# A gated unit on one core: three slots packed in place, one instruction per tile and engine, and small stores at the start

## Chip, cores and metric

One core of a Trainium2 chip. The metric is the device time of one execution in microseconds (us), the median of several runs. The profile comes from one traced execution; its span is about 2 us shorter than the time.

## The reference

```python
x = np.random.randn(8192, 8192).astype(np.float32)

def reference(x):
    a, b = np.split(x, 2, axis=-1)
    return a * (1 / (1 + np.exp(-b)))
```

268 MB are read and 134 MB written; there is one sigmoid and one multiply per result. Nothing is read twice.

## The kernel before

The 8192 rows are cut into 32 tiles. A tile has two rows per partition: 64 KB per partition in, 32 KB out. Loads are issued by SyncE (SP). Stores are issued by ScalarE (ACT), whose queue also holds the sigmoids. VectorE (DVE) multiplies.

```python
R = 2
pool = ctx.enter_context(tc.tile_pool(name="io", bufs=2))
for i in range(n_tiles):
    x_sb = pool.tile([P, R * n_cols], fp32)
    o_sb = pool.tile([P, R * half], fp32)
    load = nc.sync.dma_start(out=x_sb, in_=x_t[i])
    n = 4 if i == n_tiles - 1 else 1        # the last tile in pieces
    w = half // n
    for r in range(R):
        for c in range(n):
            ...                             # a, b: one row's halves; cols: its place in o_sb
            nc.scalar.activation(out=b, in_=b, func=SIG)
            nc.vector.tensor_mul(out=o_sb[:, cols], in0=a, in1=b)
            if n > 1:
                nc.scalar.dma_start(out=out_t[i, :, cols], in_=o_sb[:, cols])
    if n == 1:
        nc.scalar.dma_start(out=out_t[i], in_=o_sb)
```

The order in which instructions stand in each engine's queue is made by a scheduler from this program; it need not be the program's order. At the end the first load is moved into the entry block.

Of the kernel before, what the change touches and what calls it, by code (L numbers as in the profile page):

```python
# [1 line left out]

# [4 lines left out]


def _tiles(ctx, tc, x, out):
    nc = tc.nc  # L10
    P = nc.NUM_PARTITIONS
    fp32 = mybir.dt.float32
    SIG = mybir.ActivationFunctionType.Sigmoid

    n_rows, n_cols = x.shape
    half = n_cols // 2
    R = 2
    n_tiles = n_rows // (P * R)
    x_t = x.rearrange("(n p r) m -> n p (r m)", p=P, r=R)
    out_t = out.rearrange("(n p r) m -> n p (r m)", p=P, r=R)  # L20

    pool = ctx.enter_context(tc.tile_pool(name="io", bufs=2))
    first = None

    for i in range(n_tiles):
        x_sb = pool.tile([P, R * n_cols], fp32)
        o_sb = pool.tile([P, R * half], fp32)
        load = nc.sync.dma_start(out=x_sb, in_=x_t[i])
        first = first or load
        n = 4 if i == n_tiles - 1 else 1  # L30
        w = half // n
        for r in range(R):
            for c in range(n):
                lo = r * n_cols + c * w
                a = x_sb[:, lo : lo + w]
                b = x_sb[:, lo + half : lo + half + w]
                cols = slice(r * half + c * w, r * half + (c + 1) * w)
                nc.scalar.activation(out=b, in_=b, func=SIG)  # L38
                nc.vector.tensor_mul(out=o_sb[:, cols], in0=a, in1=b)  # L39
                if n > 1:  # L40
                    nc.scalar.dma_start(out=out_t[i, :, cols], in_=o_sb[:, cols])  # L41
        if n == 1:
            nc.scalar.dma_start(out=out_t[i], in_=o_sb)
    return first


@with_exitstack
def kernel(
    ctx: ExitStack,
    tc: tile.TileContext,  # L50
    x: bass.AP,
    out: bass.AP,
):



    nc = tc.nc
    with ExitStack() as pools:
        _tiles(pools, tc, x, out)
    tc.close()  # L60
    tc.compile()  # L61
    blocks = nc.main_func.blocks
    entry, body = blocks[0].instructions, blocks[1].instructions
    SP = mybir.EngineType.SP
    at = next(k for k, i in enumerate(body) if i.engine == SP)
    load = body[at]
    assert load.opcode == "DMACopy" and not load.sync_info.on_wait
    del body[at]
    where = next(k for k, i in enumerate(entry) if i.engine == SP and i.opcode == "Drain")
    entry.insert(where, load)  # L70


# [1 line left out]
_INS = ['x']  # L74
_OUTS = [((8192, 4096), 'float32')]


# [23 lines left out]
```

## Time and profile before

| | before |
|---|---|
| time, median of 6 runs | 936.12 us (935.98 to 937.0) |
| span of the profiled run | 933.9 us |
| DMA engines busy, loads + stores | 66.5% + 33.3% |
| VectorE, ScalarE busy | 30%, 25% |
| rate in the steady part | 434 GB/s |

The first thing to read is the DMA row, which says 9 in every slice. The kernel is a copy with a little arithmetic beside it, and the only time to be won is that in which the 16 DMA engines are not at full rate. The prediction shows the lines.

### The profile page before, as it was taken

The page shows a single profiled execution, that of the slowest core. Times are in us where ns is not written, and L with a number is a line of the kernel's source. Part 1 is how long each engine was busy: PE and PEld are TensorE (multiplying, and loading weights), DVE is VectorE, ACT ScalarE, POOL GpSimd, SP SyncE. Part 2 cuts the span into 40 slices and gives each one's busy share as a digit, 9 for nine tenths or more (in the row PEclk, how much of TensorE's full clock was granted, in tenths as well). Part 3 has the DMA queues.
Part 4 walks back from the last instruction along what each step waited for, and adds up shares of the span by engine and source line. Part 5 has one row for each costly group of instructions (what it writes and reads, how often), then busy time and mean ns, then how long its engine had stood idle before and what let it go on. Part 6 is the DMA issues. An engine that isn't in the chain of part 4 may idle for free.

```text
span 933.9 us, 410 instructions
## 1 busy us (share of the span) xinstructions
DVE 280.9 (30%) x70; ACT 230.0 (25%) x71; POOL 0.2 (0%) x4
## 2 busy tenths in 40 slices
DVE  0333321333213333133331333312333123331234
ACT  1313331133311333203332033320233202333023
POOL 0000000000000000000000000000000000000000
DMA  9999999999999999999999999999999999999998
GB/s 404 420 434 431 453 418 429 439 434 449 420 456 404 452 424 427 449 425 451 412 459 410 438 438 425 451 421 452 413 449 421 431 445 443 429 420 453 410 446 362
DMA packets 10226, 402.67 MB, mean 431 GB/s; under 512 B 1136, under 2 KB 1136, under 8 KB 2160
## 3 DMA queue, kind: packets, MB, share of 16 engines
q1 hardware_dynamic: 4608, 268.44, 66.5%
q10 hardware_dynamic: 5616, 134.22, 33.3%
q14 instruction: 2, 0.02, 0.0%
HBM read 268.44 MB, written 134.22 MB: 431 GB/s over the span
## 4 chain that ended last, share of the span: by engine, by line
DMA 78%; DVE 15%; ACT 6%; issue 0%; DVEq 0%; ACTq 0%
DMA x_sb<-in_x_dram 78%; DVE o_sb L39 15%; ACT x_sb L38 6%; DVEq L61 0%; ACTq L41 0%; ACTq L38 0%
## 5 line engine op out<-in xcount | busy, mean ns | idle before, releaser
L39 DVE TENSOR_TENSOR o_sb<-x_sb 128x4096 f32<-128x4096 f32 (+1 forms) x70 | 280.9, 4056 | 647.2 <-ACT x_sb L38 647.2
L38 ACT ACTIVATE x_sb<-x_sb 128x4096 f32<-128x4096 f32 (+1 forms) x70 | 228.7, 3315 | 695.9 <-DMA x_sb<-in_x_dram 691.8
L38 ACT ACT_TABLE_LOAD x1 | 1.3, 1283 | 0.8 <-PEq L85 0.8
L85 POOL MEMSET const-uint8-127<- 128x1 uint8 x1 | 0.1, 103 | 0.0
L85 POOL MEMSET const-bfloat16-1.0<- 128x1 bf16 x1 | 0.1, 102 | 0.0
L85 POOL MEMSET const-float32-0.0<- 128x1 f32 x1 | 0.1, 99 | 0.2 <-issue 0.2
L85 POOL MEMSET const-float32-1.0<- 128x1 f32 x1 | 0.1, 99 | 0.0
## 6 DMA issues: line engine op xcount, KB each, us to landing
out_dram<-o_sb ACTq DMA_DIRECT2D x31, 4096.0 KB, 41.7
out_dram<-o_sb ACTq DMA_DIRECT2D x8, 512.0 KB, 6.2
x_sb<-in_x_dram SPq DMA_DIRECT2D x32, 45.5
```

The source lines that it names most:

```text
L38: nc.scalar.activation(out=b, in_=b, func=SIG)
L39: nc.vector.tensor_mul(out=o_sb[:, cols], in0=a, in1=b)
L85: nc = _bacc.Bacc("TRN2", target_bir_lowering=False, num_devices=1)
```

## The change

The intent: a single 64 KB slot per partition holds a tile's input and, packed into its first half, its result, so that three tiles fit where two pairs of buffers did; each tile has one sigmoid and one multiply; 128 KB of small stores go out at the start, so that the store queue is in use until the first result is ready; the last tile is loaded in halves and stored in larger pieces.

```diff
-    pool = ctx.enter_context(tc.tile_pool(name="io", bufs=2))
+    pool = ctx.enter_context(tc.tile_pool(name="slots", bufs=1))
+    slots = [pool.tile([P, R * n_cols], fp32, name=f"slot{k}") for k in range(SLOTS)]
+    def implied(later, *earlier):            # drops a wait that follows from another
+        for e in earlier:
+            tc.declare_no_dep(later.ins, e.ins, reason="follows from the wait that is kept")
+    nc.vector.memset(blank, 0.0)
+    nc.scalar.dma_start(
+        out=out_t[n_tiles - 1, :, :256].rearrange("p (k m) -> p k m", k=2),
+        in_=blank.to_broadcast([P, 2, 128]))
...
+        rows = slot.rearrange("p (r h m) -> p r h m", r=R, h=2)
+        packed = slot[:, : R * half].rearrange("p (r m) -> p r m", r=R)
+        def load(cols):
+            ins = nc.sync.dma_start(out=slot[:, cols], in_=x_t[i, :, cols])
+            implied(ins, *(e for e in gone if e not in awaited))   # awaited: the slot's last stores
+        def glu(r, c):
+            sig = nc.scalar.activation(out=rows[:, r, 1, c], in_=rows[:, r, 1, c], func=SIG)
+            mul = nc.vector.tensor_mul(out=packed[:, r, c], in0=rows[:, r, 0, c], in1=rows[:, r, 1, c])
+            implied(sig, *gone); implied(mul, *gone, *now["loads"])
+            if i == n_tiles - 1:
+                tc.keep_in_program_order(sig)
...
+        if i < n_tiles - 1:
+            load(slice(0, R * n_cols))
+            glu(slice(0, R), every)
+            ...                              # one store; two for the last tile but one
+        else:                                # last tile: two loads, row 1 in halves, two stores
```

More of the change, by code (lines that the diff above doesn't have):

```diff
@@ L13, in _tiles @@
     SIG = mybir.ActivationFunctionType.Sigmoid
+    SLOTS = 3
     n_rows, n_cols = x.shape
@@ L20, in _tiles @@
     out_t = out.rearrange("(n p r) m -> n p (r m)", p=P, r=R)
-    pool = ctx.enter_context(tc.tile_pool(name="io", bufs=2))
-    first = None
-    for i in range(n_tiles):
-        x_sb = pool.tile([P, R * n_cols], fp32)
-        o_sb = pool.tile([P, R * half], fp32)
-        load = nc.sync.dma_start(out=x_sb, in_=x_t[i])
-        first = first or load
-        n = 4 if i == n_tiles - 1 else 1
-        w = half // n
-        for r in range(R):
-            for c in range(n):
-                lo = r * n_cols + c * w
-                a = x_sb[:, lo : lo + w]
-                b = x_sb[:, lo + half : lo + half + w]
-                cols = slice(r * half + c * w, r * half + (c + 1) * w)
-                nc.scalar.activation(out=b, in_=b, func=SIG)
-                nc.vector.tensor_mul(out=o_sb[:, cols], in0=a, in1=b)
-                if n > 1:
-                    nc.scalar.dma_start(out=out_t[i, :, cols], in_=o_sb[:, cols])
-        if n == 1:
-            nc.scalar.dma_start(out=out_t[i], in_=o_sb)
@@ L44, in _tiles @@
-    return first
+    pool = ctx.enter_context(tc.tile_pool(name="slots", bufs=1))
[3 more added lines that the diff above has]
+            tc.declare_no_dep(later.ins, e.ins, reason="follows from the wait that is kept")
+    blank = ctx.enter_context(tc.tile_pool(name="blank", bufs=1)).tile([P, 1, 128], fp32)
+    nc.vector.memset(blank, 0.0)
+    nc.scalar.dma_start(
+        out=out_t[n_tiles - 1, :, :256].rearrange("p (k m) -> p k m", k=2),
+        in_=blank.to_broadcast([P, 2, 128]),
+    )
@@ new lines, in _tiles, with store @@
+    kinds = ("loads", "sigs", "muls", "stores")
+    history = [{k: [] for k in kinds} for _ in range(SLOTS)]
+    last_stores = [[] for _ in range(SLOTS)]
+    every = slice(0, half)
+    for i in range(n_tiles):
+        slot = slots[i % SLOTS]
+        old = history[i % SLOTS]
+        now = {k: [] for k in kinds}
+        gone = sum(old.values(), [])
+        awaited = last_stores[i % SLOTS]
+        rows = slot.rearrange("p (r h m) -> p r h m", r=R, h=2)
[3 more added lines that the diff above has]
+            implied(ins, *(e for e in gone if e not in awaited))
+            now["loads"].append(ins)
+        def glu(r, c):
+            sig = nc.scalar.activation(out=rows[:, r, 1, c], in_=rows[:, r, 1, c], func=SIG)
+            mul = nc.vector.tensor_mul(
+                out=packed[:, r, c], in0=rows[:, r, 0, c], in1=rows[:, r, 1, c]
+            )
+            implied(sig, *gone)
+            implied(mul, *gone, *now["loads"])
+            if i == n_tiles - 1:
+                tc.keep_in_program_order(sig)
+            now["sigs"].append(sig)
+            now["muls"].append(mul)
+        def store(cols):
+            ins = nc.scalar.dma_start(out=out_t[i, :, cols], in_=slot[:, cols])
+            implied(ins, *(e for e in gone if e not in old["stores"]), *now["loads"], *now["sigs"])
+            now["stores"].append(ins)
+        if i < n_tiles - 1:
+            load(slice(0, R * n_cols))
+            glu(slice(0, R), every)
+            n_stores = R if i == n_tiles - 2 else 1
+            w = R * half // n_stores
+            for k in range(n_stores):
+                store(slice(k * w, (k + 1) * w))
+        else:
+            for r in range(R):
+                load(slice(r * n_cols, (r + 1) * n_cols))
+            for r in range(R):
+                halves = [slice(0, half // 2), slice(half // 2, half)]
+                for c in [every] if r == 0 else halves:
+                    glu(slice(r, r + 1), c)
+                store(slice(r * half, (r + 1) * half))
+        for k in kinds:
+            old[k] += now[k]
+        last_stores[i % SLOTS] = now["stores"]
@@ L64 @@
     SP = mybir.EngineType.SP
-    at = next(k for k, i in enumerate(body) if i.engine == SP)
+    at = next(k for k, i in enumerate(body) if i.engine == SP and i.opcode == "DMACopy")
     load = body[at]
```

## The prediction

> **What bounds the kernel now.** I read the page's busy lines first, then the DMA digits, the queue table, stretches of the run one by one, and last the chain of waits.
>
> ```profile
> span 933.9 us, 410 instructions
> DVE 280.9 (30%) x70; ACT 230.0 (25%) x71; POOL 0.2 (0%) x4
> ...
> DMA  9999999999999999999999999999999999999998
> ...
> q1 hardware_dynamic: 4608, 268.44, 66.5%
> q10 hardware_dynamic: 5616, 134.22, 33.3%
> ...
> HBM read 268.44 MB, written 134.22 MB: 431 GB/s over the span
> ```
>
> VectorE and ScalarE are idle 70% of the span and more, while the 16 DMA engines are busy in every slice. The two queues' packets, loads (q1) and stores (q10), fill 66.5 + 33.3 = 99.8% of the engines' time. A kernel like this gains only if it moves fewer bytes, moves them faster, or closes the 0.2%.
>
> To see where speed is lost I cut the span at the places where the traffic changes: loads alone, loads with stores, the end. Columns: stretch, length, three engines' busy time, clock, DMA share, GB/s.
>
> ```profile
> 4.10:37.90 33.80, 8.76 (x2) 7.12 (x2) 0.00 (x0) 1.00 1.00 432
> 37.90:41.50 3.60, 0.00 (x0) 0.00 (x0) 0.00 (x0) 1.00 1.05 319
> ...
> 0.00:41.50 41.50, 8.76 (x2) 8.41 (x3) 0.20 (x4) 1.00 0.98 407
> 41.50:99.50 58.00, 17.52 (x4) 14.24 (x4) 0.00 (x0) 1.00 1.00 434
> 99.50:911.50 812.00, 245.31 (x56) 199.44 (x56) 0.00 (x0) 1.00 1.00 434
> 911.50:933.90 22.40, 9.35 (x8) 7.90 (x8) 0.00 (x0) 1.00 0.88 372
> ```
>
> Loads alone run at 432 GB/s and loads mixed with stores at 434, the same rate. A tile is 8.39 MB in and 4.19 MB out, 12.58 MB, so at 434 GB/s it takes 29.0 us, and 32 tiles take 32 x 29.0 = 928 us. The span is 933.9, so only 5.9 us are not full-rate traffic. The table says where. In the first 41.5 us, 407 GB/s moved 16.9 MB, worth 38.9 us: 2.6 us lost. In the last 22.4 us, 372 GB/s moved 8.33 MB, worth 19.2 us: 3.2 us lost. Of the first loss about 1.0 us is one event: between 37.9 and 41.5, where the first stores join the loads, the rate falls to 319, and 3.6 x (434 - 319)/434 = 0.95 us. The other 1.6 us are the issue of the first load and its slow first packets.
>
> ```profile
> 0.79 42.87 DMA x_sb<-in_x_dram
> 43.66 0.02 issue
> 43.68 3.62 ACT x_sb L38
> 47.31 0.02 issue
> 47.33 8.77 DVE o_sb L39 x2
> 56.12 45.52 DMA x_sb<-in_x_dram
> ```
>
> The chain of waits looks like a latency chain: landing, sigmoid, two multiplies, next load. It would tempt one to say that the compute, 12.4 us of every 58, is on the path. It is not. The load issued at 56.12 takes 45.5 us for bytes that take 19.3 us alone, because it stands behind other transfers; the compute is hidden behind a full DMA queue.
>
> ```profile
> out_dram<-o_sb ACTq DMA_DIRECT2D x31, 4096.0 KB, 41.7
> x_sb<-in_x_dram SPq DMA_DIRECT2D x32, 45.5
> L39 DVE TENSOR_TENSOR o_sb<-x_sb 128x4096 f32<-128x4096 f32 x62 | 271.6, 4422 | 626.6 <-ACT x_sb L38 626.6
> L38 ACT ACTIVATE x_sb<-x_sb 128x4096 f32<-128x4096 f32 x62 | 220.8, 3608 | 670.1 <-DMA x_sb<-in_x_dram 670.1
> ```
>
> **What the Trainium skill says.** "DMA: Bandwidth & Descriptors", section "Where 436 GB/s comes from", puts the ceiling of the 16 engines at 435.2 GB/s, and says that for HBM to SBUF a limit of about 358 binds first. The trace sides with the first: 434 sustained for 870 us on this lone core. The steady state therefore cannot be improved by the change; it is within 0.3% of the ceiling.
>
> The same page, section "Queues, rings and completion order", says that an engine takes turns between the rows it has work for, packet by packet. The trace agrees only in part. If turns began at issue, a 4 MB store beside loads would need about 29 us; it takes 41.7 from issue to landing. The other 13 us I read as transfers issued earlier going first. So I work the new order out first come, first served, and test the tail also with turns.
>
> "VectorE: DVE Perf Modes", section "The TRN2 errata", gives (N+151)/0.96 ns for an fp32 two-tensor operation: 4,424 for 4,096 columns, and the trace has 4,422. It also gives ScalarE 224 cycles plus one per column at 1.2 GHz: 3,600, and the trace has 3,608. I use both forms for the new sizes.
>
> **The change part by part.**
>
> One instruction per tile and engine. Sigmoid: (224 + 8192)/1.2 = 7.0 us for 2 x 3.6; multiply: (8192 + 151)/0.96 = 8.7 us for 2 x 4.42. This saves 0.2 + 0.15 us a tile, all beside DMA. But the two no longer overlap inside a tile: landing to store issue becomes 7.0 + 8.7 = 15.7 us where it was 12.4. Worth to the end: 0.
>
> Three slots instead of two pairs. The result overwrites the input, so a load now waits for the landing of the store of three tiles ago, not for a multiply. In the built order there is a further point that the diff doesn't show. From the fourth tile on, ScalarE's queue holds, for every three tiles, sigmoid a, sigmoid b, store a, store b, sigmoid c, store c. Store a thus waits until load b has landed, though its data is ready long before. Does this empty the DMA queue? I lay out one period of three tiles first come, first served, with 19.3 us per load, 9.7 per store, 1.8 from the last packet to a load's landing and 2.7 to a store's (two gaps in the trace between the last packet and the instruction that waited for it):
> - load a runs 0 to 19.3; the store of the previous c to 29.0; load b to 48.3; load c to 67.7; store a to 77.4; store b to 87.1; then the next load a.
> - load b is issued when the previous store b has landed (2.7), load c when the previous store c has (31.7), store a once load b has landed (50.1), store b 15.7 later (65.8), and the next load a when store a has landed (80.1).
>
> Each is in the queue before its turn: 26, 17, 18, 12 and 7 us ahead. There are stretches with loads alone and with stores alone, but never one with nothing, and load-only and mixed rates are equal. So the period stays 87.1 = 3 x 29.0. Worth: 0.
>
> The small stores. 128 x 256 floats are 131 KB in 512-byte pieces, 0.3 us at full rate; I estimate 0.6 as small pieces are slower (4 KB pieces ran 159 ns, 412 GB/s, at the end of this kernel). They give the store queue its first use while the engines start anyway. At best the 0.95 us at 38 us disappear. Sum: -0.95 + 0.6 = -0.35.
>
> The tail. The 4 KB pieces become 16 KB: 4.19 MB at 412 instead of 434 cost 0.5 us, saved. After the last half tile has landed come a 2,048-column sigmoid, (224 + 2048)/1.2 = 1.9 us, two multiplies of (2048 + 151)/0.96 = 2.3, issue and start about 1.5: 8.0 us. First come, first served, both halves of the last load run before the stores of the last tile but one, so up to 9.7 + 4.8 us of stores are still queued: no hole. With turns taken packet by packet only some 6 to 7 us are left, a hole of 1 to 2 us. I take +0.5 for this.
>
> Sum: 936.2 - 0.35 - 0.5 + 0.5 = 935.8 us.
>
> **Rivals.**
>
> First: the store queue, empty for long stretches because of the deferred stores, pays the 0.95 us of the first join again and again. For it: that loss stands exactly where stores join loads. Against: in the kernel before, store after store is issued and the rate stays at 434. Ten periods with one join each would make 936 + 9.5 = 945; a join per tile, 31 x 0.95, would make 965 and "slower".
>
> Second: the deferred stores drain the queue. A slot's own loop with everything shared is 29 + 29 (waiting for load b) + 29 + 2.7 = 90, over the 87 available. If loads and stores always shared, 3 us would be lost per period, 30 in all: 966. Against it: sharing is what makes these 29 and not 19.3 or 9.7, and when one queue runs dry the other runs at full rate.
>
> Third: a real gain. If the start loss fell to the first packet's 1.0 us and the end loss to a landing of 2, the span would be 931, the time 933. Below that there is only a rate over 434, and nothing in the profile offers one.
>
> **Range and chances.** The floor is 928 us of traffic plus a start, a landing and the 2.3 us between span and time, 932 to 933; being 2% faster (917.5) would need 442 GB/s with no loss at all. The upper side is open to the first two rivals in part, so the range is lopsided: 933.5 to 940. Chances: 0.01 faster, 0.95 same, 0.04 slower.
>
> **What would show each step.** Right: a steady rate of 434 in 100 to 850 us, DMA digits of 9 throughout, no drop near the first large store, stores' time to landing up and irregular with a period of three tiles. VectorE rows of about 8.7 us and ScalarE's of 7.0. Wrong: a DMA share below 0.99 in the middle, repeating every 87 us (a rival), slow packets at the start that hold the first load up beyond 22 us (the small stores cost more than they save), or an idle DMA between the last load's landing and the last store.

## The result, and the profile after

| | before | changed |
|---|---|---|
| time, median of 6 runs | 936.12 us (935.98 to 937.0) | 943.11 us (942.63 to 948.8) |
| ratio of fast runs | | 1.0084 (1.0061 to 1.0108) |
| span of the profiled run | 933.9 us | 941.0 us |

A ratio here is the mean time of one kernel's fast runs over that of the other's of the same rounds, so not quite the ratio of the medians. The kernel is 7 us slower: inside the 2% that was given 0.95, but outside the range of 933.5 to 940.

The page of the changed kernel, in the rows that answer to those of before:

```profile
span 941.0 us, 208 instructions
DVE 278.6 (30%) x35; ACT 226.5 (24%) x35; POOL 0.2 (0%) x4
...
DMA  9999999999999999999999999999999999999998
...
q1 hardware_dynamic: 4752, 268.44, 66.5%
q10 hardware_dynamic: 5168, 134.35, 33.1%
```

This page hides the loss. The DMA digits are still 9, and the queues' packets still fill 99.6% of the engines. A share of busy time can't tell a packet that moves at full rate from one that is stalled. The rate can. Stretches of the changed kernel (length, busy time of DVE, ACT and POOL, clock, DMA share, GB/s), and the steady stretch of the kernel before:

```profile
100.00:900.00 800.00, 234.70 (x27) 193.99 (x28) 0.00 (x0) 1.00 1.00 431
...
40.00:44.00 4.00, 0.00 (x0) 2.31 (x1) 0.00 (x0) 1.00 0.87 264
...
246.50:252.30 5.80, 0.00 (x0) 5.48 (x1) 0.00 (x0) 1.00 1.01 435
252.30:256.00 3.70, 2.12 (x1) 1.55 (x1) 0.00 (x0) 1.00 0.99 363
...
928.00:931.00 3.00, 2.03 (x1) 0.00 (x0) 0.00 (x0) 1.00 0.86 366
...
935.00:939.70 4.70, 0.00 (x0) 0.00 (x0) 0.00 (x0) 1.00 0.43 185
```

```profile
100.00:900.00 800.00, 245.31 (x56) 199.44 (x56) 0.00 (x0) 1.00 1.00 434
```

In the steady 800 us, 431 instead of 434 GB/s is 800 x 3/434 = 5.5 us, with the rounding of the two figures up to 1.8 us either way; summed packet by packet, load packets took 3.6 us more per engine from 100 us on. The third and fourth rows show how it is lost. From 246.5 to 252.3 the engines run at 435 and then, at the same busy share, at 363 for 3.7 us: 3.7 x (434 - 363)/434 = 0.6 us. What changes at 252.3 the DMA view of the stretch just before it shows; it lists the queues that moved anything:

```profile
DMA packets 61, 1.93 MB, mean 430 GB/s; under 512 B 2, under 2 KB 2, under 8 KB 2
...
q10 hardware_dynamic: 61, 1.93, 99.5%
```

There is no q1 row: until 252 only stores ran, and the loads' queue was dry. The slow stretch is the loads' return. Single packets in the trace say the same. A 64 KB load packet takes 2.42 us nearly everywhere in both kernels. From 100 us on the loads of the changed kernel return nine times, after 6.2 to 7.1 us in which no load packet ran. Of these 144 first packets (one for each of the 16 engines at each return) 90 took more than 0.1 us longer, 0.51 us on average, and together they make 2.9 of the 3.6 us. The other 54 were at full speed: the first two returns slow all 16 engines, most later ones 7 or 8. (Of the 80 that follow six or seven stores in a row 79 are slow; most that follow eight or more are not.) In the kernel before the loads' queue never runs dry in this way.

Seen from the issues: between 100 and 900 us 106 load packets are slow by more than 0.2 us, and 82% of them are in flight 6 us after a load was issued, about when its packets join; of the other load packets 8% are. Summed up and divided by 16 engines, load packets took 4.4 us more than before and store packets 0.5 (0.43 of it the small stores' own packets); the remaining 2.0 us are idle engines, at the end above all: some engines had lost more than others and finished last (the last row). Each engine closes a transfer with a 4-byte packet; those of the last load are spread over 7.6 us, in the kernel before over 1.7.

Why the loads' queue is dry is in the order of time. The columns are start, length, engine, line and instruction:

```profile
107.38 7.03 ACT L71 ACTIVATE slot<-slot 128x8192 f32<-128x8192 f32 x1 [28.60 <-DMA slot<-in_x_dram]
114.44 8.69 DVE L72 TENSOR_TENSOR slot<-slot 128x8192 f32<-128x8192 f32 x1 [26.94 <-ACT slot L71]
131.41 7.03 ACT L71 ACTIVATE slot<-slot 128x8192 f32<-128x8192 f32 x1 [17.00 <-DMA slot<-in_x_dram]
131.42 16.12 ACTq L83 DMA_DIRECT2D out_dram<-slot  x2
```

The multiply is done at 123.1. Its store is issued at 131.4, when the next tile's load has landed and let that tile's sigmoid pass, because the scheduler has put the store behind that sigmoid. The next load into this slot waits for this store's landing. It happens to 9 of the 32 tiles, every third from the fourth on.

The arithmetic itself came out as worked out (8,690 and 7,013 ns), which changes nothing:

```profile
L72 DVE TENSOR_TENSOR slot<-slot 128x8192 f32<-128x8192 f32 x31 | 269.5, 8692 | 641.0 <-ACT slot L71 641.0
L71 ACT ACTIVATE slot<-slot 128x8192 f32<-128x8192 f32 x31 | 217.9, 7029 | 682.1 <-DMA slot<-in_x_dram 682.1
```

### The profile page after: what moved, and what is told of

Read it like the earlier page. It is cut to its first block, busy times and chain, and to the rows that moved or that the text cites. A ratio compares the mean times of both kernels' runs of the same rounds, so it can differ in the third digit from the quotient of the medians.

```text
span 941.0 us, 208 instructions
## 1 busy us (share of the span) xinstructions
DVE 278.6 (30%) x35; ACT 226.5 (24%) x35; POOL 0.2 (0%) x4
## 4 chain that ended last, share of the span: by engine, by line
DMA 81%; DVE 9%; ACT 8%; DVEq 0%; issue 0%; SPq 0%
DMA slot<-in_x_dram 43%; DMA out_dram<-slot 38%; DVE slot L72 9%; ACT slot L71 8%; DVEq L121 0%; SPq L66 0%
## 5 line engine op out<-in xcount | busy, mean ns | idle before, releaser
L72 DVE TENSOR_TENSOR slot<-slot 128x8192 f32<-128x8192 f32 (+2 forms) x34 | 278.4, 8190 | 650.6 <-ACT slot L71 650.6
L71 ACT ACTIVATE slot<-slot 128x8192 f32<-128x8192 f32 (+2 forms) x34 | 225.2, 6627 | 699.2 <-DMA slot<-in_x_dram 689.6
```

The costliest lines, as they stand in the source:

```text
L71: sig = nc.scalar.activation(out=rows[:, r, 1, c], in_=rows[:, r, 1, c], func=SIG)
L72: mul = nc.vector.tensor_mul(out=packed[:, r, c], in0=rows[:, r, 0, c], in1=rows[:, r, 1, c])
```

## The experiments

All kernels gave correct results. Times beside each other come from the same chip, where the kernel before stood at 936.08 to 936.25. A first build of e1 and of two kernels like it was refused by the race check before the chip: holding only the sigmoids let the scheduler move the last tile's second load ahead; in the kernels below that load is held too. The theories: A, the store held back behind a sigmoid lets the loads' queue run dry, and the return costs; U, as A, for the return of either queue; B, the small stores cost; C, waiting for a store's landing costs in any order.

**e1_in_order.** Every sigmoid keeps its place, so no store is held back.

```diff
-            if i == n_tiles - 1:
-                tc.keep_in_program_order(sig)
+            tc.keep_in_program_order(sig)
```

> The changed kernel with every sigmoid held in program order, so that no store stands behind the next tile's sigmoid. Theory A (the deferred store lets the load queue run dry once every three tiles, some engines' next load packets then take 0.3 to 1.3 us longer, and the engines that lose most set the end): the repeated slow load packets go, 937 +-1.5 us. Theory B (the small stores at the start cost the time): no change, 942 to 944. Theory C (a load that waits for a store's landing runs the queue dry in any order of issue): no change, 941 to 944, with slow load packets still there every 87 us.

936.44 us, ratio to the kernel before 1.0001 (0.9989 to 1.0013). The whole loss is gone. The same tile in order of time:

```profile
107.42 7.03 ACT L73 ACTIVATE slot<-slot 128x8192 f32<-128x8192 f32 x1 [28.83 <-DMA slot<-in_x_dram]
114.48 8.69 DVE L74 TENSOR_TENSOR slot<-slot 128x8192 f32<-128x8192 f32 x1 [27.16 <-ACT slot L73]
123.21 0.34 ACTq L84 DMA_DIRECT2D out_dram<-slot  x1
```

The store goes out 8.2 us earlier, and that is all it takes. After 80 us no engine has a dry loads' queue for more than a packet or two, and the slow packets are gone apart from single ones:

```profile
100.00:900.00 800.00, 239.25 (x28) 196.81 (x28) 0.00 (x0) 1.00 1.00 433
```

One return is left, at 75 us, with 1.0 us on average, before the rhythm has settled. Theories B and C fall for this kernel.

**e2_no_small.** The small stores and their memset are taken out of the changed kernel.

```diff
-    blank = ...; nc.vector.memset(blank, 0.0)
-    nc.scalar.dma_start(out=out_t[n_tiles - 1, :, :256]..., in_=blank.to_broadcast([P, 2, 128]))
```

> The changed kernel without the small stores. Theory A: they only cost their own packets, about 0.4 us per engine, so 942 to 943. Theory B: 936 to 938. If they do what they are meant for (spare the stall where the first large store joins the loads), it is 0.5 to 1 us slower than the changed kernel, 943.5 to 944.5.

942.5 us, 1.0066 (1.0051 to 1.0081). The loss stands without them, and they don't spare the stall where the first large store joins: without them the load packets at 40 us take 1.01 us longer, with them 1.02. Its loads return nine times too, after 6.9 to 7.0 us without them, and here all 144 first packets are slow, by 0.40 us on average.

**e5_in_order_no_small.** Both edits at once.

> Both undone at once: sigmoids in program order and no small stores; three slots in place and the new tail stay. Theory A: 0.4 us under the run with order alone, 936 to 937. Theory C: 941 to 943. If order and small stores each carry a part, this run alone comes down to 936 and the two single ones lie between.

936.38 us, 0.9998 (0.9985 to 1.0011): the small stores make no difference that these runs can see in the kernel with its stores in order.

**e3_before_small.** The kernel before with the small stores alone.

```diff
+    nc.vector.memset(blank, 0.0)
+    nc.scalar.dma_start(out=out_t[n_tiles - 1, :, :256]..., in_=blank.to_broadcast([P, 2, 128]))
```

> The kernel before with only the small stores added. Theory A: 936 to 937, ratio 1.000 to 1.001. Theory B: 940 or more. If the small stores spare the stall of the first large store: 935.0 to 935.6.

942.53 us, 1.0074 (1.0043 to 1.0105), against what theory A expected. Here the small stores do cost, by another way: no queue runs dry. The engines run a load and a store packet in turn, and both of a pair end together, where in the kernel before the stores start two packets ahead and end earlier. The loss begins in the middle of the run.

**e10_before_small_again.** The same kernel, since that profile had fallen on a run of 954 us.

> The kernel before with the small stores once more, because the profile of the first time fell on a run of 954 us. If its slow load packets in the second half, with loads and stores alternating one for one and no queue ever dry, belong to the kernel: 940 to 943 us with such packets, fewer of them. If they belong to that one run: 940 to 943 us with the loss somewhere else.

945.28 and 938.83 us, 1.006 (1.0027 to 1.0093). The profiled run, a fast one, has the same picture, later: full rate up to 757 us, then 24 to 37 load packets in every 29 us that take 0.5 to 0.7 us longer. It belongs to the kernel.

**e8_before_half_small.** 8 small packets per engine in the kernel before, where there were 16.

```diff
-        out=out_t[n_tiles - 1, :, :256].rearrange("p (k m) -> p k m", k=2), in_=blank.to_broadcast([P, 2, 128]),
+        out=out_t[n_tiles - 1, :, :128].rearrange("p (k m) -> p k m", k=1), in_=blank,
```

> The kernel before with 8 small packets per engine where 16 were added: they end at about 21 us, well before the first large store. With 16 they ran until the first large store, whose packets then began behind a load instead of two ahead and ended together with the load's, and the time rose to 942. If this shift of the rhythm is what costs: the two-ahead start comes back and the time is 936.2 to 937. If small stores as such cost: 939 or more.

935.54 us, 0.9998 (0.9986 to 1.001). Eight packets per engine cost nothing, so small stores as such don't. Sixteen last until the first large store; that the packets' turn then differs is seen in the trace. That this turn is what costs is not shown: e13 below runs one for one and ends pairs together as well, and keeps its rate.

**e4_half_order.** Half the dose: sigmoids held in every second group of three, 5 stores held back instead of 9.

```diff
-            if i == n_tiles - 1:
+            if i == n_tiles - 1 or i // SLOTS % 2:
                 tc.keep_in_program_order(sig)
```

> The changed kernel with the sigmoids of every second group of three tiles held in program order: 5 stores stand behind the next tile's sigmoid where 9 did. Theory A (each deferred store makes one load-queue restart, and each restart costs): a part of the loss, 936.4 + 6.5 x 5/9 = 940 +-1 us, and the repeated slow load packets about 5 times. If the pattern of deferral as such, or leaving the strict rhythm once, costs all of it: 942.5 or more.

940.45 us, 1.0056 (1.0042 to 1.0071). The median lies between the two, as a cost for each held-back store asks, but the interval overlaps that of the changed kernel (1.0061 to 1.0108), so this run alone doesn't show it. Its trace, taken in one of its slower runs (942.98), fits theory A only in part: the slow packets come in five groups, as expected, but of the 64 first packets of its four returns after 100 us only 25 are slow, and they carry 0.75 of the 5.0 us that its load packets lost from 100 us on. More are slow where stores join loads that had run alone: 44% of the slow packets are in flight 3.5 us after a store's issue, against 10% of the others.

**e6_split_restart.** e5, with the fourth tile's load split so that the half that the store doesn't hold goes first. It was meant to remove the return at 75 us and to beat the kernel before.

```diff
+            if i == SLOTS:
+                load(slice(n_cols, R * n_cols), old["muls"])   # needs the multiply alone
+                load(slice(0, n_cols))                         # needs the store's landing
```

> Sigmoids in order, no small stores, and the load of the fourth tile (the only one that finds the load queue dry at about 75 us in the run in order) split: its second half, which only the multiply of the first tile has to free, goes ahead, its first half waits for the store. Theory A: the restart at 75 us, about 1.05 us of slow loads and 0.3 of slow stores on average over the engines, goes, 935.0 +-0.5 us, under the kernel before. If what happens at 75 us comes from the first stores and not from the dry load queue: no change, 936.4.

936.63 us, 1.0009 (0.9997 to 1.0021): missed. The return at 75 us is gone and one at 164 us has come for it, with 1.0 us of slow loads:

```profile
157.50:163.50 6.00, 0.00 (x0) 5.22 (x1) 0.00 (x0) 1.00 1.05 415
163.50:168.00 4.50, 2.66 (x1) 1.81 (x1) 0.00 (x0) 1.00 1.00 342
```

Stores alone, then the loads' return. So it isn't tied to the first stores; both kernels with their sigmoids in order have one such event before the rhythm settles, e6 only later.

**e7_deferred_not_dry.** The changed kernel, stores still held back, but every load into the first slot split as in e6.

```diff
+            if i >= SLOTS and i % SLOTS == 0:
+                load(slice(n_cols, R * n_cols), old["muls"])
+                load(slice(0, n_cols))
```

> The changed kernel with its deferred stores and small stores left as they are, but every load into the first slot split in two, the half that only the multiply has to free first, so that the load queue does not run dry though the store is as late as before. Theory A: 936.5 to 938 us (0.7 us for smaller load packets included) and no store-only stretches. If the late store itself, or the long stretches of loads alone, cost the time and not the dry load queue: 942 to 944.

946.91 us, 1.0111 (1.009 to 1.0132): a clear miss for theory A in its narrow form. The store-only stretches are gone, few load packets follow five or more stores, and load packets still took 5.5 us more per engine than before. Two stretches of this run:

```profile
916.00:923.80 7.80, 6.88 (x1) 0.00 (x0) 0.00 (x0) 1.00 0.29 124
...
218.00:226.00 8.00, 1.11 (x1) 6.86 (x1) 0.00 (x0) 1.00 0.97 385
```

The first is a fault of the experiment: loads now run so far ahead that the last ones land with no store left in the queue, 7.8 x (434 - 124)/434 = 5.6 us. The second may be the same cause seen from the other side. Loads had run alone from 199 to 222, and load packets are slow just where the stores come back: 8 x (434 - 385)/434 = 0.9 us. It looks like the stall that every kernel here has once, where the first large store joins. Of the slow 64 KB packets of this run 51% are in flight 4 us after a store's issue, against 6% of the others. So it isn't the loads' queue alone: load packets can be slow where transfers of either queue join.

**e9_in_order_dry.** The opposite: stores in order (e1), and the loads' queue made dry on purpose. A one-column copy on GpSimd ties each load into the first slot to the landing of the load before it.

```diff
+            if i >= SLOTS and i % SLOTS == 0:
+                src = slots[(i - 1) % SLOTS]
+                nc.gpsimd.tensor_copy(out=slot[:, R * n_cols - 1 :], in_=src[:, n_cols : n_cols + 1])
```

> The changed kernel in program order (936.4 us before), so with no deferred store, but every load into the first slot is also held until the load before it has landed, so that the load queue is dry for some microseconds once every three tiles while stores still run. Theory U (what costs is the return of a queue that had been empty while the other ran on: some engines' load packets take 0.3 to 1.3 us longer at each return): slow first loads again after 5 to 7 stores in a row, about ten times, 940 to 944 us. The stores may just run out before the load's first packet; idle engines would add to that and are counted apart. If the late store itself is what costs: 936.5 to 937.5 plus the idle time seen.

939.11 us, 1.0022 (1.0008 to 1.0036), with no more idle engine time than before (3.6 us on average in both). The dry queue was made as meant: 144 load packets after 100 us follow five to seven stores in a row. But only one of them is slow. This does not refute theory U, because the second half of its condition failed: the stores ran out, as the expectation had feared. After eight of the nine returns only 4 to 9 store packets start within 10 us, on all engines together; in the changed kernel it is 24 to 40. The DMA view shows it, first e9 after its return at 255 us (259 to 269 us), then the changed kernel after its return at 252 (256 to 266 us):

```profile
q1 hardware_dynamic: 66, 4.33, 99.8%
q10 hardware_dynamic: 4, 0.00, 0.0%
```

```profile
q1 hardware_dynamic: 48, 3.15, 73.6%
q10 hardware_dynamic: 37, 1.21, 28.1%
```

The four packets of q10 in e9 are the 4-byte ends. The remaining return, at 167 us, has 19 store packets and the one slow load packet. Before 100 us e9 has one return where the stores did run on, at 77 us with 32 store packets: all 16 first packets are slow, by 0.94 us on average. The other slow packets of this run sit where stores join: 68% of those from 100 us on are in flight 5 us after a store's issue, against 8% of the others, and of some 50 load packets that end seven loads in a row when a store joins, 38 are slow. So the loads' return from a dry queue does not cost by itself, where the stores have ended; load packets are slow where one queue joins the other, at some of the joins.

**e11_before_single.** The kernel before with one sigmoid and one multiply per tile, nothing else.

```diff
+        if n == 1:
+            nc.scalar.activation(out=xv[:, :, 1, :], in_=xv[:, :, 1, :], func=SIG)
+            nc.vector.tensor_mul(out=ov, in0=xv[:, :, 0, :], in1=xv[:, :, 1, :])
+            nc.scalar.dma_start(out=out_t[i], in_=o_sb)
+            continue
```

> The kernel before with one sigmoid and one multiply per tile, nothing else changed (no tile in place, two buffers of each kind). The built order now holds back 8 stores behind the next tile's sigmoid, as in the changed kernel, which the kernel before never does. If the held-back store is what costs, wherever the buffers are: 940 to 945 us with slow load packets. If it costs only with three slots in place: 936 to 937 us.

948.0 us, 1.0132 (1.0117 to 1.0147). The part that I had put down as worth nothing makes the scheduler hold back stores by itself (seven large ones in the trace, where the expectation says 8), and costs more than the whole change:

```profile
100.00:900.00 800.00, 234.70 (x27) 195.33 (x28) 0.00 (x0) 1.00 1.00 431
922.00:940.00 18.00, 9.35 (x8) 7.90 (x8) 0.00 (x0) 1.00 0.70 285
```

The steady part loses what it loses in the changed kernel, here without long stretches of one queue, and its 117 slow packets don't gather in the first 12 us after an issue (15% at most); 44% are in flight 17 us after a load's issue, against 9% of the others, and which join that is, if one, was not worked out. The stretch at the end loses 18 x (434 - 285)/434 = 6.2 us. In the trace this goes back to one engine: it falls behind the 15 others from about 214 us on and ends its share of the last load at 923.3 us, where they had ended theirs by 914.0. The last tile's sigmoid can't start before that load has landed, at 923.8, and from 924 on most engines have run out of work.

**e13_before_single_in_order.** e11 with the sigmoids held.

```diff
-            nc.scalar.activation(out=xv[:, :, 1, :], in_=xv[:, :, 1, :], func=SIG)
+            tc.keep_in_program_order(nc.scalar.activation(out=xv[:, :, 1, :], in_=xv[:, :, 1, :], func=SIG))
```

> The same with the sigmoids held in program order, so that no store is held back. One instruction per tile alone, as I had worked it out: 936.2 +-0.5 us. If fewer, longer instructions cost by themselves (store issue 3.3 us later after a landing): 938 or more.

937.94 us, 1.0019 (1.0006 to 1.0031). I did not hold all the last tile's sigmoids, and the store of the last tile but one still went behind a sigmoid of the last tile; this makes a hole before the end:

```profile
100.00:900.00 800.00, 243.30 (x28) 196.81 (x28) 0.00 (x0) 1.00 1.00 433
911.50:914.50 3.00, 0.08 (x1) 1.17 (x2) 0.00 (x0) 1.00 0.46 197
```

3 x (434 - 197)/434 = 1.6 us of the 1.8 lost are this one held-back store. (By packets, each engine stands idle for about 2 us there, and in the kernel before not at all.) The single instructions as such are worth about nothing, as worked out.

**e12_before_tail.** The kernel before with the new treatment of the last two tiles (the edit in words).

```diff
-        n = 4 if i == n_tiles - 1 else 1
+        # last tile: load in two halves, row 1 computed in halves; last two tiles: one 2 MB store per row
```

> The kernel before with the changed kernel's last two tiles: last load in two halves, stores of 2 MB. My step for the tail was 0.5 us saved by larger store pieces against a hole of up to 1 to 2 us: 935.7 to 937. In the changed kernel the hole was about 0.6 us per engine on average, at 929 to 931 us; the same here would give 936.2 to 936.8.

935.83 us, 0.9995 (0.9981 to 1.0008): a gain too small to see.

No version beats the kernel before clear of noise; the lowest, e8 and e12, are within 0.6 us of it. With 928 us of traffic at 434 GB/s there is hardly anything left to win.

## Why the prediction was wrong

- **Bound: right.** The DMA queue bounds every kernel here, and no run sustained more than 434 GB/s over the 800 us from 100 to 900.
- **One instruction per tile: sizes right, worth wrong.** 7.0 and 8.7 us were met to 20 ns. "all beside DMA" and "Worth to the end: 0" hold only for the durations (e13). The same edit changes the scheduler's order, and that costs 11.8 us in e11. I had seen the order and had treated it as a matter of the slots.
- **Three slots and held-back stores: the step that failed.** It said: "There are stretches with loads alone and with stores alone, but never one with nothing, and load-only and mixed rates are equal. So the period stays 87.1 = 3 x 29.0. Worth: 0." The queue indeed was never empty. But a full queue is not yet full rate: with the stores held back, load packets are slowed where the loads return and the stores run on, 90 of 144 by 0.51 us each, and the engines get out of step. The period, from the sigmoids at 131.4 and 832.6 us, was 87.65 us, against 87.0 in e1. So "load-only and mixed rates are equal" holds, but not for the changes between them. Removing the held-back stores gave all 7 us back (e1); that half as many cost half is not shown (e4).
- **The first rival was nearest.** It had the cost, "the 0.95 us of the first join again and again", and a figure for ten of them, 945. I set it aside because store after store is issued in the kernel before without loss. That compared the wrong thing: there neither queue is ever absent for long. It also named the stores' queue; in the changed kernel it is mostly the loads' that returns. Nor does every join cost: 54 of 144 first packets were at full speed.
- **The small stores: wrong.** "At best the 0.95 us at 38 us disappear": they did not. The changed kernel still falls to 264 GB/s at 40 to 44 us. Their cost in it is not visible (e1 beside e5), while in the kernel before they cost 6 us by a way that stays open (e3, e10).
- **Order of service: partly wrong.** I worked it out first come, first served for whole transfers. In the trace the first large store, issued at 38 us, alternates from 44 us on with a load issued at 1 us, packet by packet. Only what was already next in line, some 6 us, went ahead of it. The layout therefore had each queue alone for far longer than the measured 6 us or so of stores alone.
- **Tail: right in size.** -0.5 and +0.5 were predicted, -0.3 measured alone and within noise (e12). The hole in the changed kernel was there, 3 x (434 - 366)/434 = 0.5 us; the larger loss at the end is the engines' being out of step after unequal stalls.
- **Range: too narrow above.** The chance of "same" was right; the rivals' part was said to be open above, and 940 did not leave it the 7 us that it took. (The 442 GB/s asked for 917.5 us comes out at 440, from 402.65 MB in 917.5 - 2.3 us; nothing rests on it.)

What is shown and what stays open: that the held-back stores cause the loss is shown by e1, e11 and e13; that the loss in the steady part lies in slow load packets is read from the packets of every slow run. What makes a load packet slow is not settled. The changed kernel, e2, e4, e7 and e9 have them where one queue joins the other, but not on every engine; the kernel before issues a load and a store every 29 us with only single ones after the first store; and for e11 no join was found that they go with. Theory U fits them best, and fits the one return that e1, e5 and e9 have near 76 us with their stores in order (15 or 16 of 16 first packets slow), but no run tested it by itself, so it stands as a reading of the traces and not as shown. Why 16 small stores disturb the kernel before from the middle of the run on is open too.

## What to carry to other kernels

In a kernel that is bound by DMA, look at what the scheduler did to the queue that issues the stores: a store that stands behind the next tile's compute is late by that tile's load, even where its own data is long ready, and merging instructions can bring this about. Hold the order and measure before crediting or blaming buffers. And don't read a DMA share of 99% as full rate: compare GB/s in long stretches, and look at the time that single packets take, and at whether all engines end a transfer together.

## What the Trainium skill lacked or had wrong

- "DMA: Bandwidth & Descriptors", section "Where 436 GB/s comes from", lets about 358 GB/s bind transfers between HBM and SBUF; a lone core sustained 434 for 800 us in both directions mixed, and 432 for loads alone. (The 425 that the same section calls near fabric-rate is closer.)
- The same page, "Queues, rings and completion order", has engines take turns by packet. It lacks that a transfer issued while the other queue is busy joins only 3 to 7 us later (a load issued at 248.0 us had its first packets at 252.3 us), and that load packets can be slowed then: by 0.51 us on average in 90 of 144 first packets where the changed kernel's loads return, by 0.8 to 1.2 us where the first large store joins in every kernel. In e9, where the stores had run out, 143 of 144 first packets were at full speed.
- The same page, "Specifications", gives 512 B as the least size for line rate; the 512-byte packets of the small stores took 27 ns, 19 GB/s per engine, against 27 for the 64 KB load packets (65,536 B in 2.42 us).
- No page says that a core's own loads and stores can put its DMA engines out of step, or what that costs: in the changed kernel the engines ended the last load up to 7.6 us apart and the rate fell to 185 GB/s from 935.0 to 939.7 us; in e11 one engine was 9 us behind.
